# Squared deviation from the row mean: two whole-tile stores, and the sums and squares of a tile shared differently between ScalarE and VectorE

## The chip, the cores and the metric

The kernel runs on one core of a Trainium2 chip. The metric is the time of one execution in device microseconds (us), as the median of several runs; the kernel before takes 83.28 us (median of four runs, 83.21 to 83.51).

Four parts of the core matter here. VectorE (DVE) and ScalarE (ACT) compute on tiles in the on-chip memory. The queue of SyncE (SP) issues the transfers between main memory and that memory; an issue can wait for semaphores first, and what stands behind it in the queue waits with it. Sixteen DMA engines carry the transfers out. Each of them takes packets from the queue in order; here a packet is one contiguous run of one partition.

## The reference

The input `x` has 1024 rows of 4096 float32. From every element the mean of its row is subtracted, and the difference is squared. The output has the same shape and type, so 16.78 MB are read and 16.78 MB are written.

```python
def reference(x: np.ndarray, axis: int) -> np.ndarray:
    mean = np.mean(x, axis=axis, keepdims=True)
    return ((x - mean) ** 2).astype(np.float32)
```

## The kernel before

The 1024 rows are cut into two tiles of 512 rows. In a tile each of the 128 partitions holds Q = 4 consecutive rows, 16384 float32 or 64 KiB, contiguous in main memory too. Both tiles stay in the on-chip memory for the whole kernel (`io`, two buffers), so no transfer waits for a buffer.

The SP queue issues both loads at the start (L43), each of 128 runs of 64 KiB. Then a Python loop, unrolled when the program is built, goes over the two tiles and over the four rows `q` of each:

- L51, VectorE: the negated sum of the row (`neg_sum`, one value per partition).
- L54, VectorE: the sum times 1/4096 gives `neg_mean`.
- L55, ScalarE: the row is overwritten by the square of (row + `neg_mean`).
- L64, SP queue: after every second row, the store of two rows, 128 runs of 32 KiB; four stores in all, of 4 MiB each.

VectorE and ScalarE run their instructions in the order in which the program has them. A scheduler works that order out when the program is built: it puts the sum of the next row ahead of the small L54 of the row before, so that VectorE streams sums back to back and L54 never waits for the sum directly in front of it. The SP queue has the order load, load, store, store, store, store. The store of rows 0 and 1 waits for ScalarE's second square, that of rows 2 and 3 for the fourth. Both tiles are treated alike; the second one's work starts when its load has landed.

Of the kernel before, what the change touches and what calls it, by code (L numbers as in the profile page):

```python
# [2 lines left out]

os.environ.setdefault("NEURON_RT_ULTRASERVER_MODE", "4")

# [4 lines left out]

F32 = mybir.dt.float32


@with_exitstack
def kernel(
    ctx: ExitStack,
    tc: tile.TileContext,
    x: bass.AP,
    axis: bass.AP,
    out: bass.AP,  # L20
):


    nc = tc.nc

    B, D = x.shape
    P = nc.NUM_PARTITIONS
    Q = 4
    H = 2
    assert B % (P * Q) == 0  # L30
    ntiles = B // (P * Q)
    inv_d = 1.0 / float(D)

    x_t = x.rearrange("(n p q) d -> n p (q d)", p=P, q=Q)
    out_t = out.rearrange("(n p q) d -> n p (q d)", p=P, q=Q)

    io = ctx.enter_context(tc.tile_pool(name="io", bufs=ntiles))
    stats = ctx.enter_context(tc.tile_pool(name="stats", bufs=2 * ntiles * Q))

    tiles = []  # L40
    for i in range(ntiles):
        x_tile = io.tile([P, Q * D], F32)
        nc.sync.dma_start(out=x_tile, in_=x_t[i])  # L43
        tiles.append(x_tile)

    for i in range(ntiles):
        for q in range(Q):
            row = tiles[i][:, q * D:(q + 1) * D]
            neg_sum = stats.tile([P, 1], F32)
            neg_mean = stats.tile([P, 1], F32)  # L50
            nc.vector.reduce_sum(  # L51
                out=neg_sum, in_=row, axis=mybir.AxisListType.X, negate=True
            )
            nc.vector.tensor_scalar_mul(out=neg_mean, in0=neg_sum, scalar1=inv_d)  # L54
            nc.scalar.activation(  # L55
                out=row,
                in_=row,
                func=mybir.ActivationFunctionType.Square,
                bias=neg_mean,
                scale=1.0,  # L60
            )
            if q % H == H - 1:
                part = slice((q + 1 - H) * D, (q + 1) * D)
                nc.sync.dma_start(out=out_t[i][:, part], in_=tiles[i][:, part])  # L64


# [1 line left out]
_INS = ['x', 'axis']  # L68
_OUTS = [((1024, 4096), 'float32')]

_NUMBERS = {'axis': -1}


# [26 lines left out]
```

## Time and profile before

| What | us |
|---|---|
| median of four runs | 83.28 |
| the profiled execution | 83.33 |
| its span, first to last instruction | 81.5 |
| outside the span in the profiled execution | 1.8 |
| VectorE busy | 35.4 |
| ScalarE busy | 30.7 |
| one row's sum on VectorE (128x4096) | 4.411 |
| one row's square on ScalarE (128x4096) | 3.704 |
| L54 on VectorE (128x1) | 0.146 |
| issue of the two loads on the SP queue | 0.73 to 1.58 |
| first load landed (VectorE begins) | 22.71 |
| second load landed (VectorE begins again) | 42.03 |
| issue of the four stores | 39.68, 47.66, 59.00, 66.98 |

Times within the span count from its first instruction. The profile lists for each engine how long it was busy, and for the DMA queue how many packets it moved and which share of the sixteen engines' span these took. A group of instructions is given with its line, its engine, what it writes and reads, its shape, its count and its mean duration. The timeline lists the instructions in order with their starts, and in square brackets how long an engine stood idle before one of them and what ended the wait. The chain of work that ended last is followed back from the last instruction by the semaphores, as far as these show.

The trace also has a record of every single DMA packet, with its start, duration and size. These records are told here in words: the 256 packets of 64 KiB are those of the loads, the 512 of 32 KiB those of the stores, and 96 packets of 4 bytes report the end of a transfer, one for each of the six transfers on each of the sixteen engines.

### The profile page before, as it was taken

Reading aid. Unit: us, or ns where it says so; the run is one execution under the profiler, and the core shown is the slowest. Engines: PE = TensorE matmul, PEld = TensorE weight load, DVE = VectorE, ACT = ScalarE, POOL = GpSimd, SP = SyncE. Lnnn points to the kernel's source line nnn. Section 1 sums busy time; section 2 is a strip of 40 time slices with the busy share of each in tenths; the row PEclk is TensorE's granted clock in tenths of the full one; section 3 lists DMA queues with packets and bytes.
Section 4 is the critical chain, followed back from the end, with each engine's and each line's share of the span. In section 5 each row is a group of like instructions: output and inputs, shape, how many; then the busy total and the mean of one; then the engine's idle time right before and its main releaser. Section 6 shows DMA issues by size and latency. Waiting matters only on the chain.

```text
span 81.5 us, 79 instructions
## 1 busy us (share of the span) xinstructions
DVE 35.4 (43%) x16; ACT 30.7 (38%) x9; POOL 0.2 (0%) x4
## 2 busy tenths in 40 slices
DVE  0000000000089999999839999999930000000000
ACT  0000000000060005969699930978979980000000
POOL 0000000000000000000000000000000000000000
DMA  9599957999974999992997998998999899799790
GB/s 321 193 514 514 482 225 321 514 514 514 514 321 193 514 514 514 514 482 96 450 498 321 466 514 354 418 514 370 402 514 418 354 514 450 322 514 466 321 498 0
DMA packets 864, 33.55 MB, mean 411 GB/s; under 512 B 96, under 2 KB 96, under 8 KB 96
## 3 DMA queue, kind: packets, MB, share of 16 engines
q1 hardware_dynamic: 864, 33.55, 96.0%
HBM read 16.78 MB, written 16.78 MB: 411 GB/s over the span
## 4 chain that ended last, share of the span: by engine, by line
DMA 50%; DVE 22%; ACT 5%; ACTq 4%; SPq 0%; issue 0%
DMA x_tile<-in_x_dram 50%; DVE neg_sum L51 21%; ACT x_tile L55 5%; ACTq L95 4%; SPq L43 0%; DVE neg_mean L54 0%
## 5 line engine op out<-in xcount | busy, mean ns | idle before, releaser
L51 DVE TENSOR_REDUCE neg_sum<-x_tile 128x1 f32<-128x4096 f32 x8 | 35.0, 4411 | 24.3 <-DMA x_tile<-in_x_dram 24.3
L55 ACT ACTIVATE x_tile<-x_tile,neg_mean 128x4096 f32<-128x4096 f32 x8 | 29.4, 3704 | 13.5 <-DVE neg_mean L54 13.5
L55 ACT ACT_TABLE_LOAD x1 | 1.3, 1283 | 22.8 <-DMA x_tile<-in_x_dram 22.8
L54 DVE TENSOR_SCALAR neg_mean<-neg_sum 128x1 f32<-128x1 f32 x8 | 1.1, 146 | 0.0
L81 POOL MEMSET const-bfloat16-1.0<- 128x1 bf16 x1 | 0.1, 102 | 0.0
L81 POOL MEMSET const-uint8-127<- 128x1 uint8 x1 | 0.1, 102 | 0.0
L81 POOL MEMSET const-float32-0.0<- 128x1 f32 x1 | 0.1, 99 | 0.2 <-issue 0.2
L81 POOL MEMSET const-float32-1.0<- 128x1 f32 x1 | 0.1, 99 | 0.0
## 6 DMA issues: line engine op xcount, KB each, us to landing
out_dram<-x_tile SPq DMA_DIRECT2D x4, 4096.0 KB, 12.9
x_tile<-in_x_dram SPq DMA_DIRECT2D x2, 31.4
```

Source lines behind the costliest of these rows:

```text
L51: nc.vector.reduce_sum(out=neg_sum, in_=row, axis=mybir.AxisListType.X, negate=True)
L54: nc.vector.tensor_scalar_mul(out=neg_mean, in0=neg_sum, scalar1=inv_d)
L55: nc.scalar.activation(out=row, in_=row, func=mybir.ActivationFunctionType.Square, bias=neg_mean, scale=1.0,)
L81: nc = _bacc.Bacc("TRN2", target_bir_lowering=False, num_devices=1)
L95: with _tile.TileContext(nc) as tc:
```

## The change

The four stores become two. Each takes a whole tile of 8 MiB, in 128 runs of 64 KiB, and waits until all four rows of the tile are done.

The rows of a tile are shared out anew. Rows 0, 1 and 2 are summed on VectorE as before. Row 3 is summed on ScalarE: an Identity activation copies the row into a scratch buffer and adds it up (`accum_out`), and a second small activation multiplies the total by -1/4096. ScalarE then squares row 3, row 0, row 1 and the first half of row 2. VectorE squares the second half of row 2 in two passes over 2048 elements per partition: an addition of the negated mean (`tensor_scalar_add`), then a multiplication of the result with itself (`tensor_mul`).

The instructions marked `inorder` are kept in the order of the program. On VectorE each small multiplication by 1/4096 now stands directly behind the sum that it needs, and waits for it. The load of ScalarE's function table, which waited for the first tile's load in the kernel before, has no such wait after the change.

```diff
-    H = 2
+    H = D // 2
...
+    scratch = ctx.enter_context(tc.tile_pool(name="scratch", bufs=1))
...
+    inorder = tc.keep_in_program_order
+
+    def mean_on_act(row):
+        copy = scratch.tile([P, D], F32)
+        total = stats.tile([P, 1], F32)
+        neg_mean = stats.tile([P, 1], F32)
+        nc.scalar.activation(
+            out=copy, in_=row, func=ACT.Identity, scale=1.0, accum_out=total
+        )
+        nc.scalar.mul(out=neg_mean, in_=total, mul=-inv_d)
+        return neg_mean
+
+    def mean_on_dve(row):
+        neg_sum = stats.tile([P, 1], F32)
+        neg_mean = stats.tile([P, 1], F32)
+        inorder(nc.vector.reduce_sum(
+            out=neg_sum, in_=row, axis=mybir.AxisListType.X, negate=True
+        ))
+        inorder(nc.vector.tensor_scalar_mul(out=neg_mean, in0=neg_sum, scalar1=inv_d))
+        return neg_mean
+
+    def square_on_act(part, neg_mean):
+        inorder(nc.scalar.activation(
+            out=part, in_=part, func=ACT.Square, bias=neg_mean, scale=1.0
+        ))
+
     for i in range(ntiles):
-        for q in range(Q):
-            row = tiles[i][:, q * D:(q + 1) * D]
...
-            if q % H == H - 1:
-                part = slice((q + 1 - H) * D, (q + 1) * D)
-                nc.sync.dma_start(out=out_t[i][:, part], in_=tiles[i][:, part])
+        row = [tiles[i][:, q * D:(q + 1) * D] for q in range(Q)]
+        m3 = mean_on_act(row[3])
+        m0 = mean_on_dve(row[0])
+        square_on_act(row[3], m3)
+        m1 = mean_on_dve(row[1])
+        square_on_act(row[0], m0)
+        m2 = mean_on_dve(row[2])
+        square_on_act(row[1], m1)
+        square_on_act(row[2][:, :H], m2)
+        back = row[2][:, H:]
+        nc.vector.tensor_scalar_add(out=back, in0=back, scalar1=m2)
+        nc.vector.tensor_mul(out=back, in0=back, in1=back)
+        nc.sync.dma_start(out=out_t[i], in_=tiles[i])
```

More of the change, by code (lines that the diff above doesn't have):

```diff
@@ L11 @@
 F32 = mybir.dt.float32
+ACT = mybir.ActivationFunctionType
 @with_exitstack
@@ L44 @@
         tiles.append(x_tile)
-    for i in range(ntiles):
-        for q in range(Q):
-            row = tiles[i][:, q * D:(q + 1) * D]
[L49 to L61, printed above, removed]
-            if q % H == H - 1:
-                part = slice((q + 1 - H) * D, (q + 1) * D)
-                nc.sync.dma_start(out=out_t[i][:, part], in_=tiles[i][:, part])
+    inorder = tc.keep_in_program_order
[20 more added lines that the diff above has]
+        ))
+    for i in range(ntiles):
+        row = [tiles[i][:, q * D:(q + 1) * D] for q in range(Q)]
[11 more added lines that the diff above has]
+        nc.sync.dma_start(out=out_t[i], in_=tiles[i])
 _INS = ['x', 'axis']
```

## The prediction

> **What bounds the kernel now.** I read the page first: the engines' busy times beside the share of the DMA queue.
>
> ```profile
> span 81.5 us, 79 instructions
> ...
> DVE 35.4 (43%) x16; ACT 30.7 (38%) x9; POOL 0.2 (0%) x4
> ...
> DMA  9599957999974999992997998998999899799790
> ...
> DMA packets 864, 33.55 MB, mean 411 GB/s; under 512 B 96, under 2 KB 96, under 8 KB 96
> ...
> q1 hardware_dynamic: 864, 33.55, 96.0%
> ```
>
> Neither compute engine is busy for half of the span. The packets fill 96.0% of sixteen engines' time, and what is missing lies at the two ends: no packet starts before 1.7 us, and none runs after 80.4. The dips in the row of digits come from long packets being counted by their ends. The stretches with loads alone and with stores alone show that neither direction is slacker:
>
> ```profile
> 2.00:41.00 39.00, 17.71 (x8) 9.37 (x4) 0.00 (x0) 1.00 0.96 413
> 41.70:80.40 38.70, 17.71 (x8) 20.66 (x6) 0.00 (x0) 1.00 0.97 420
> ```
>
> (The columns are the stretch, its length, the busy times of VectorE, ScalarE and GpSimd, the clock, the DMA share and GB/s.) The records of single packets settle it: on each of the sixteen engines the next packet starts within some nanoseconds of the end of the one before, from the first load to the last store, also where a load passes into a store and one store into the next. So the DMA engines set the end, and computation counts only where it lets them run dry. The chain of waits on the page names DVE for 22%, because it follows semaphores and can't see that the stores stood queued.
>
> The third view is the timeline around the first store, for how nearly that happens:
>
> ```profile
> 22.71 8.74 DVE L51 TENSOR_REDUCE neg_sum<-x_tile 128x1 f32<-128x4096 f32 x2 [22.71 <-DMA x_tile<-in_x_dram]
> ...
> 35.82 4.41 DVE L51 TENSOR_REDUCE neg_sum<-x_tile 128x1 f32<-128x4096 f32 x1
> 35.94 3.71 ACT L55 ACTIVATE x_tile<-x_tile,neg_mean 128x4096 f32<-128x4096 f32 x1 [0.68 <-DVE neg_mean L54]
> 39.68 0.35 SPq L64 DMA_DIRECT2D out_dram<-x_tile  x1
> 40.15 0.27 DVE L54 TENSOR_SCALAR neg_mean<-neg_sum 128x1 f32<-128x1 f32 x2
> 40.33 3.71 ACT L55 ACTIVATE x_tile<-x_tile,neg_mean 128x4096 f32<-128x4096 f32 x1 [0.68 <-DVE neg_mean L54]
> 42.03 4.42 DVE L51 TENSOR_REDUCE neg_sum<-x_tile 128x1 f32<-128x4096 f32 x1 [1.61 <-DMA x_tile<-in_x_dram]
> ```
>
> The first store is issued at 39.68. The DMA engines finish their last load packets between 41.13 (the earliest) and 41.67 (the latest), and find store packets waiting. From the first load's issue at 0.73 to its first packet at 1.73 it took 1.00 us; for the first store it can't have been more than 41.13 - 39.68 = 1.45, as no engine stood still. I take 1.00, the only direct row, and keep 1.45 as the other end.
>
> **The stores themselves.** A load packet of 64 KiB starts 2.414 us after the one before it (median of the records), a store packet of 32 KiB 1.2095 us. Two of these make 2.419, so a 64 KiB store packet should save 0.005 if writing goes like reading. An engine carries 32 store packets now and 16 afterwards: 16 x 0.005 = 0.08. Two end reports fewer per engine, 0.006 each, bring the gain to 0.09. Two issues fewer on SP (0.34 each) gain nothing, as they lie beside running packets. As bounds: zero gain if writes have no cost per packet, and 16 x 1% of 2.414 = 0.39 lost, were long writes 1% slower than long reads; 413 against 420 GB/s in the rows above gives no hint of that.
>
> The Trainium skill speaks for far more. Its page "DMA: Bandwidth & Descriptors", section "Anatomy of one DMA — SWDGE (gpsimd) path", fits a DMA's time with a fixed 2.0 us plus its bytes, which for two stores fewer would be 4.0 us and 79.3 in all. That fit is for single transfers of another queue; here stores follow each other on an engine without a gap, so the fixed part is hidden, and I don't count it.
>
> **When the tile is released: VectorE.** It starts the first tile at 22.71. Each sum takes 4.41. The L54 behind it now waits for it: in the rows above the second one of the pair at 40.15 starts at 40.27, 0.04 after its sum's end (35.82 + 4.41 = 40.23). The next sum starts 0.06 after L54's start (31.38 to 31.44, 35.76 to 35.82). So the pitch grows to 4.41 + 0.04 + 0.06 = 4.51, where it was 4.38. The third sum ends at 22.71 + 2 x 4.51 + 4.41 = 36.14, and its mean is there 0.20 later, at 36.34 (0.04 wait, 0.15 run, 0.01 semaphore). The fourth sum, 4.4, is gone. Then come two instructions of 128x2048 that the trace doesn't have. The multiplication reads two operands and goes by the sum's row: 0.146 fixed (the 128x1 row) and 2048/4096 of the remaining 4.265, 2.28. The addition is a TENSOR_SCALAR, known only at 128x1 with 0.146; its upper end is the sum's rate again, 2.28. The two rows are equally near, one by the operation, the other by length, so I take the middle, 1.21, and keep both. Release by VectorE: 36.34 + 0.03 + 1.21 + 0.03 + 2.28 = 39.89.
>
> By the skill's page "VectorE: DVE Perf Modes", section "The perf-mode tier table (the rule you actually need)", an fp32 tensor_scalar of 2048 elements takes 1.227 us and a tensor_tensor 2.293. That would move the release by 0.03 and the total by nothing; no row here shows it.
>
> **ScalarE.** The table load (1.28) no longer waits for the first tile, and either way lies beside a sum. From 22.74: the Identity with its sum takes between 3.71 (a square) and 4.41 (VectorE's sum); I take 3.86, a square with one 128x1 instruction (0.146) on top for the total. The small multiplication lies between 0.146 (VectorE's 128x1) and 1.28 (the longest other ACT row); I take 0.20 with its wait, near the row of its shape. From 26.60 and 26.80, and with a wait of 0.03, the square of row 3 ends at 30.54. Rows 0 and 1 follow in 3.61 each (two squares take 7.31 where one takes 3.71, an overlap of 0.10), since their means are there by 27.3 and 31.8: 37.76. The half square, 0.146 + half of 3.56 = 1.93 less the overlap, ends at 39.59. The scheduler's order of the built program agrees: row 3, 0, 1, half of 2.
>
> **Sum.** The store is issued when the later engine is done, at 39.91, 0.23 after the first store of before, and its packets are ready at 40.91. The earliest DMA engine comes free at 41.13, the latest at 41.67. Nothing runs dry; the slack of the engine that ends last is 0.76. The second tile repeats it: it starts at 42.03 and takes the same 17.20, so its store is issued at 59.23, ready at 60.23; the first store's sixteen engines need 8 x 2.414 + 0.006 = 19.32 from 41.13 to 41.67, that is to 60.45 and 60.99. The slack is the same 0.76, and a delay in both tiles counts once, since a late first store moves the second one's deadline by as much. The extra waits (SP on both engines instead of one, L54 behind its sum) hold up nothing but this. So the last packet ends 0.09 before 80.40, the span, 81.54 to two places, becomes 81.45, and with the 1.79 around it the profiled execution is 83.24 instead of 83.33. That execution lay 0.05 above the median of the four runs, so for the median I predict 83.28 - 0.09 = 83.20, rounded: 0.1% less, which a measurement will hardly tell from nothing (about 0.3%, or 0.25 us, is what it tells).
>
> **Rival 1, slower: the tile is released late and the queue runs dry.** Before, half a tile was enough to start; now the longest of two chains must end. The place is the first store packet; it decides from a release after 41.67 - 1.00 = 40.67, 0.76 later than my sum, and from there each us counts in full. It exceeds 0.3% from a release after 41.01. ScalarE's upper ends (0.55 + 1.08 more) give 39.59 + 1.63 + 0.02 = 41.24, 0.57 lost, less the 0.09 gained: 83.76. The addition at its upper end gives a release at 40.98, 0.31 lost, 83.50; with an issue-to-packet time of 1.45 too, 83.95. Against it: all three values must lie near their upper ends, and an addition of up to 1.97 costs nothing.
>
> **Rival 2, faster: a store has a fixed cost that the packet records don't show.** If each dropped store gave back its issue on SP, 0.34, the time would be 82.5 with the 0.09. Against it: no gap between stores.
>
> **Rival 3, slower: long writes go worse than long reads.** At 1%: 0.39 more, 83.67. For it speaks only that no 64 KiB write is in the trace; against it, that reading 64 KiB and writing twice 32 KiB agree within 0.2%.
>
> **Rival 4: the stores don't get longer runs.** If the queue cuts a row into packets of 32 KiB, only four end reports are saved: 83.27. The loads' packets have 64 KiB, so I doubt it.
>
> **How the numbers follow.** Forecast 0.66, rival 1 0.17, rival 2 0.07, rival 3 0.04, rival 4 0.06. Faster by over 0.3%: rival 2, 0.07. Within: forecast and rival 4, 0.72. Slower: rivals 1 and 3, 0.21. The forecast's own range is 83.05 to 83.45, by the scatter of the runs (0.07 below and 0.23 above their median). To leave out no more than 2 in 10 the range goes on to the middle of rivals 1 and 3: 83.02 to 83.75.
>
> **What would show it.** After the change there should be 576 packets (256 + 256 + 64), two stores issued near 39.9 and 59.2, DVE busy 2 x (3 x 4.41 + 3 x 0.15 + 3.49) = 34.3, ACT about 35.4, and a DMA share of 96%. ScalarE and VectorE should end a tile within some 0.3 of each other. I am wrong if the first store is issued after 40.7, if a store packet of 64 KiB takes other than 2.42, or if the span moves with the queue still full.

## The result and the profile after

The changed kernel takes 83.50 us (median of 44 runs, 83.26 to 83.71); the kernel before, run beside it, 83.31 (67 runs). The ratio is 1.0022, with a 95% interval of 1.0017 to 1.0028: slower by 0.19 us, where 0.09 less was forecast. The time lies in the range given, but the sign is wrong, and many runs resolve it.

The page of the changed kernel:

```profile
span 81.7 us, 81 instructions
...
DVE 34.2 (42%) x16; ACT 34.7 (42%) x15; POOL 0.2 (0%) x4
...
DMA packets 576, 33.55 MB, mean 411 GB/s; under 512 B 64, under 2 KB 64, under 8 KB 64
...
q1 hardware_dynamic: 576, 33.55, 95.7%
...
L87 DVE TENSOR_TENSOR x_tile<-x_tile 128x2048 f32<-128x2048 f32 x2 | 4.6, 2293 | 0.1
L86 DVE TENSOR_SCALAR x_tile<-x_tile,neg_mean 128x2048 f32<-128x2048 f32 x2 | 2.6, 1286 | 0.1
```

The packets are the 576 expected, so the runs did become longer, and the engines are busy for the times that were worked out (34.3 and 35.4 expected). The DMA queue is still the bound, but its share fell from 96.0 to 95.7% while the span grew. The timeline of the first tile's end and the second tile's start:

```profile
26.56 12.80 ACT L71 ACTIVATE x_tile<-x_tile,neg_mean 128x4096 f32<-128x4096 f32 x4
...
36.06 0.15 DVE L67 TENSOR_SCALAR neg_mean<-neg_sum 128x1 f32<-128x1 f32 x1
36.25 1.29 DVE L86 TENSOR_SCALAR x_tile<-x_tile,neg_mean 128x2048 f32<-128x2048 f32 x1
37.58 2.29 DVE L87 TENSOR_TENSOR x_tile<-x_tile 128x2048 f32<-128x2048 f32 x1
39.95 0.35 SPq L88 DMA_DIRECT2D out_dram<-x_tile  x1
41.91 3.62 ACT L55 ACTIVATE copy<-x_tile 128x4096 f32<-128x4096 f32 x1 [2.56 <-DMA x_tile<-in_x_dram]
```

VectorE ends the tile at 39.87 and ScalarE at 39.36; the store is issued at 39.95 against 39.91 in the forecast. The computation did what was worked out. What differs stands in the records of the single packets around 41 us. On the sixteen engines the last load packet ends at 41.10 to 41.53, and the first store packet starts at 41.30 to 41.74. The records don't name the engine, so which start follows which end is certain only where packets stand back to back; the mean standstill does not depend on it. It is 0.21 here. Before it was 0.03: fourteen engines went on within some nanoseconds, and two stood still for about 0.2 each. From there to the last packet, end reports included, 64 KiB of store take 2.4234 on average, against 2.4223 before (pairs of 32 KiB) and 2.414 forecast. The second store shows no such gap.

So in these two executions the engines end on average at 80.24 instead of 80.11. The gap gives +0.18, the store packets 16 x 0.001 = +0.02, and a load that happened to end 0.07 earlier takes that off again. The last packet ends at 80.52 instead of 80.40, which is the 0.12 between the two profiled executions (83.45 and 83.33).

### The profile page after: what moved, and what is told of

It reads as the page before. It is cut to its first block, busy times and chain, and to the rows that moved or that the text cites. A ratio compares the mean times of both kernels' runs of the same rounds, so it can differ in the third digit from the quotient of the medians.

```text
span 81.7 us, 81 instructions
## 1 busy us (share of the span) xinstructions
DVE 34.2 (42%) x16; ACT 34.7 (42%) x15; POOL 0.2 (0%) x4
## 3 DMA queue, kind: packets, MB, share of 16 engines
q1 hardware_dynamic: 576, 33.55, 95.7%
## 4 chain that ended last, share of the span: by engine, by line
DMA 50%; DVE 21%; SPq 0%; issue 0%
DMA x_tile<-in_x_dram 50%; DVE neg_sum L64 16%; DVE x_tile L87 3%; DVE x_tile L86 2%; DVE neg_mean L67 1%; SPq L46 0%
## 5 line engine op out<-in xcount | busy, mean ns | idle before, releaser
L64 DVE TENSOR_REDUCE neg_sum<-x_tile 128x1 f32<-128x4096 f32 x6 | 26.5, 4413 | 24.6 <-DMA x_tile<-in_x_dram 24.6
L71 ACT ACTIVATE x_tile<-x_tile,neg_mean 128x4096 f32<-128x4096 f32 (+1 forms) x8 | 25.6, 3270 | 0.1
L55 ACT ACTIVATE copy<-x_tile 128x4096 f32<-128x4096 f32 x2 | 7.2, 3617 | 23.1 <-DMA x_tile<-in_x_dram 23.1
L87 DVE TENSOR_TENSOR x_tile<-x_tile 128x2048 f32<-128x2048 f32 x2 | 4.6, 2293 | 0.1
L86 DVE TENSOR_SCALAR x_tile<-x_tile,neg_mean 128x2048 f32<-128x2048 f32 x2 | 2.6, 1286 | 0.1
```

The costliest lines, as they stand in the source:

```text
L55: nc.scalar.activation(out=copy, in_=row, func=ACT.Identity, scale=1.0, accum_out=total)
L64: inorder(nc.vector.reduce_sum(out=neg_sum, in_=row, axis=mybir.AxisListType.X, negate=True))
L71: inorder(nc.scalar.activation(out=part, in_=part, func=ACT.Square, bias=neg_mean, scale=1.0))
L86: nc.vector.tensor_scalar_add(out=back, in0=back, scalar1=m2)
L87: nc.vector.tensor_mul(out=back, in0=back, in1=back)
```

## The experiments

In what follows, the gap is this mean standstill of a DMA engine between its last load packet and its first store packet. The hold is the mean time by which the load's last packet exceeds 2.418, the duration of a load packet in full flow. Both are from the packet records of one execution. Diffs are against the changed kernel unless said otherwise; unchanged lines are left out.

### Release and packet length taken apart

Four kernels. The first keeps the release of the whole tile and shortens the runs.

```diff
-        nc.sync.dma_start(out=out_t[i], in_=tiles[i])
+        for part in (slice(2 * D, 4 * D), slice(0, 2 * D)):
+            nc.sync.dma_start(out=out_t[i][:, part], in_=tiles[i][:, part])
```

> The changed kernel, but each tile is stored by two stores of 32 KiB runs, rows 2 and 3 first, both issued when all four rows are done: the release stays where it is in the changed kernel (about 39.95 us), only the packets are shorter. Theory 'late' (the queue runs dry before the first store's packets arrive): the gap of 0.05 to 0.42 us on the DMA engines ahead of the first store stays, and so does the time, 83.45 to 83.5 us (at most 0.05 less, by 16 packets of 64 KiB at 2.423 us against pairs of 32 KiB at 2.420). Theory 'long' (the longer write packets cost the time): the time falls back to that of the kernel before, 83.3 us.

Measured: 83.66 us, ratio 1.0047 (1.0034 to 1.0059).

```profile
40.01 0.82 SPq L89 DMA_DIRECT2D out_dram<-x_tile  x2
```

The gap stays, 0.20. The short packets cost 2.4335 per 64 KiB, more than the long ones. The length of the runs is thus not what made the change slower; at an equal release it saves 0.16 us, by the medians and by the packets (16 x 0.010).

The second releases rows 0 and 1 as soon as they are done:

```diff
-        nc.sync.dma_start(out=out_t[i], in_=tiles[i])
+        for part in (slice(0, 2 * D), slice(2 * D, 4 * D)):
+            nc.sync.dma_start(out=out_t[i][:, part], in_=tiles[i][:, part])
```

> The changed kernel's sharing of sums and squares, but rows 0 and 1 are stored when they are done (about 37.5 us) and rows 2 and 3 after that, in runs of 32 KiB. Theory 'late': no gap is left on any DMA engine, 83.2 to 83.3 us, not slower than the kernel before. Theory 'long': 83.3 us too. A third theory, 'contention' (ScalarE and VectorE working at once, with an addition that reads and writes on VectorE, slow the transfers): 83.5 us, since the computation is the changed kernel's.

Measured: 84.17 us, ratio 1.0110 (1.0096 to 1.0124). No theory had this. The third has long runs with an early release, by leaving row 2 unsquared:

```diff
-        square_on_act(row[2][:, :H], m2)
-        back = row[2][:, H:]
-        nc.vector.tensor_scalar_add(out=back, in0=back, scalar1=m2)
-        nc.vector.tensor_mul(out=back, in0=back, in1=back)
```

> The changed kernel without the squares of row 2 (left out on both engines, so row 2 is stored unsquared): whole-tile stores with runs of 64 KiB, released at about 37.5 us instead of 39.95. Theory 'late': the gap ahead of the first store is gone and 83.25 to 83.35 us are left, with at most 0.05 from the longer packets. Theory 'long': 83.5 us, as in the changed kernel.

Measured: 84.13 us, ratio 1.0105 (1.0087 to 1.0123). The gaps are gone in both runs (0.003 and 0.002), as 'late' expected, and yet both lose 0.9 us. The timeline shows where: the second load lands later, though nothing was done to it. For the run with short stores:

```profile
37.66 2.80 SPq L89 DMA_DIRECT2D out_dram<-x_tile  x2
42.85 3.62 ACT L55 ACTIVATE copy<-x_tile 128x4096 f32<-128x4096 f32 x1 [3.33 <-DMA x_tile<-in_x_dram]
```

and for the one with long stores:

```profile
37.65 0.35 SPq L84 DMA_DIRECT2D out_dram<-x_tile  x1
42.85 3.62 ACT L55 ACTIVATE copy<-x_tile 128x4096 f32<-128x4096 f32 x1 [5.22 <-DMA x_tile<-in_x_dram]
```

The store is issued 2.3 us earlier, and the second tile starts at 42.85 instead of 41.91. In the packet records one packet per engine is long, the load's last one: 3.29 and 3.25 on average instead of 2.42, a hold of 0.87 and 0.83. All packets before it have their normal length. The store packets after it run better than in any other kernel so far: 2.415 per 64 KiB in long runs, which is what the loads take. 'Contention' falls too, since the third kernel does less computation than the changed one and is as slow as the second.

The fourth releases later, by one more pass over the half row:

```diff
         nc.vector.tensor_mul(out=back, in0=back, in1=back)
+        nc.vector.tensor_scalar_add(out=back, in0=back, scalar1=0.0)
```

> The changed kernel with one more VectorE instruction per tile ahead of the store (adding 0.0 to the half row that it squared), 1.3 us: the release moves from 39.95 to about 41.25 us in the first tile, and as much in the second. Theory 'late': the queue is dry already, so all of it counts, once and not twice: 83.5 + 1.3 = 84.8 us, with gaps of 1.35 to 1.7 us ahead of the first store and none ahead of the second. Theory 'long': there is slack left before the release decides, so clearly less than 1.3 us is added, 83.5 to 84.3 us.

Measured: 84.04 us, ratio 1.0092 (1.0079 to 1.0105), 0.54 more than the changed kernel instead of 1.3.

```profile
41.14 0.35 SPq L89 DMA_DIRECT2D out_dram<-x_tile  x1
41.83 3.62 ACT L55 ACTIVATE copy<-x_tile 128x4096 f32<-128x4096 f32 x1 [2.54 <-DMA x_tile<-in_x_dram]
```

The store is issued when the engines are about to fall idle, and its first packets start 0.85 to 1.00 later. In the changed kernel it was issued while the engines carried the load, and its packets started 1.35 to 1.80 after the issue, although every engine was free by 1.59. So the way from issue to packet was longer where the engines were busy, and of 1.20 us of later release only 0.58 shows as a longer gap. The time lies in the range that 'long' had named, but not for its reason: no slack was left, as every engine stands still in the changed kernel already. The delay counts once, as forecast: no gap stands ahead of the second store.

### Where the best moment lies

The theories were mended to 'arrival': a store that comes early holds the load, one that comes late leaves a gap. Four more releases. The first is a complete kernel that only balances the two engines:

```diff
-    H = D // 2
+    H = 2304
```

> The changed kernel with row 2 cut at 2304 instead of 2048, so that VectorE squares 1792 elements and ScalarE 2304: both end at about 39.6 us instead of 39.36 (ScalarE) and 39.88 (VectorE), and the store is issued near 39.6, where the first store of the kernel before stood (39.68). It computes everything. Theory 'arrival': the packets of a store reach a busy DMA engine 1.35 to 1.8 us after its issue; if that lies past the load's end (41.1 to 41.5 us) the queue runs dry, if it lies well within the load's last packet that packet is held up by about 0.9 us, and the least is lost where the two meet. By it the gaps of the changed kernel go to 0 to 0.1 us and the store packets come at 2.414 to 2.420 us: 83.2 to 83.35 us. Rival 'long': 83.5 us as before this edit.

Measured: 83.22 us, ratio 0.9988 (0.9977 to 0.9999), beside 83.29 for the kernel before.

```profile
39.87 0.35 SPq L88 DMA_DIRECT2D out_dram<-x_tile  x1
42.18 3.62 ACT L55 ACTIVATE copy<-x_tile 128x4096 f32<-128x4096 f32 x1 [2.33 <-DMA x_tile<-in_x_dram]
```

The next three leave squares out to move the release:

```diff
-        square_on_act(row[1], m1)
-        square_on_act(row[2][:, :H], m2)
-        back = row[2][:, H:]
-        nc.vector.tensor_scalar_add(out=back, in0=back, scalar1=m2)
-        nc.vector.tensor_mul(out=back, in0=back, in1=back)
```

> The changed kernel without the squares of rows 1 and 2 (both stored unsquared): the store is issued at about 33.9 us in the first tile, so its packets arrive at 35.3 to 35.7, two packets ahead of the load's last one. Theory 'arrival': what is held up is the load packet in flight when the store arrives, so now it is one that starts at 33.8 to 36.9, and the loss is about 0.9 us again, 84.1 us. Rival 'order': the load's last packet is held up because a store stands behind it, whenever that came; then the packet that starts at 38.7 to 39.3 is long, the others not; the time is 84.1 us by this too, and the packet tells.

Measured: 84.48 us, ratio 1.0150 (1.0128 to 1.0172). The packets that start at 33.7 to 34.4, in flight when the store arrives, take 2.42 to 2.43. The long one is again the load's last, which starts at 38.6 to 39.3: hold 1.18. So not the packet that meets the store is held, but the last one before it, and more the longer the store has stood there: 'order' in place of 'arrival'.

```diff
-        back = row[2][:, H:]
-        nc.vector.tensor_scalar_add(out=back, in0=back, scalar1=m2)
-        nc.vector.tensor_mul(out=back, in0=back, in1=back)
```

> The changed kernel without the square of the second half of row 2 (stored unsquared): the store is issued when ScalarE is done, at about 39.4 us. Theory 'arrival': its packets come at 40.75 to 41.2 us, near the load's end: little held up, 83.2 to 83.4 us. Rival 'step' (a store that arrives anywhere in the load's last packet costs the same): 84.1 us.

Measured: 83.20 us, ratio 0.9989 (0.9978 to 0.9999). And with `row[2][:, :1024]` squared on ScalarE in place of `row[2][:, :H]`:

> As the run with the store at 39.4 us, but ScalarE squares only the first 1024 elements of row 2: the store is issued at about 38.5 us, its packets come at 39.85 to 40.3 us, in the middle of the load's last packet. Theory 'arrival' with a cost that falls towards the load's end: 83.5 to 83.9 us. Rival 'step': 84.1 us.

Measured: 83.82 us, ratio 1.0063 (1.0041 to 1.0085). The step is refuted; the hold falls towards the load's end. The rows of the timelines for 34.03, 38.59 and 39.39 (issue of the first store, and start of the second tile, in three kernels):

```profile
34.03 0.35 SPq L83 DMA_DIRECT2D out_dram<-x_tile  x1
43.07 3.62 ACT L55 ACTIVATE copy<-x_tile 128x4096 f32<-128x4096 f32 x1 [9.06 <-DMA x_tile<-in_x_dram]
```

```profile
38.59 0.35 SPq L85 DMA_DIRECT2D out_dram<-x_tile  x1
42.50 3.62 ACT L55 ACTIVATE copy<-x_tile 128x4096 f32<-128x4096 f32 x1 [3.94 <-DMA x_tile<-in_x_dram]
```

```profile
39.39 0.35 SPq L85 DMA_DIRECT2D out_dram<-x_tile  x1
42.04 3.62 ACT L55 ACTIVATE copy<-x_tile 128x4096 f32<-128x4096 f32 x1 [2.67 <-DMA x_tile<-in_x_dram]
```

The earlier the store, the later the second tile. All of it in one table, in us. The lead is from the issue of the first store to the mean end of the load, the hold taken off; the sixth column is the mean time of 64 KiB of store. All columns but the last are from one profiled execution each, the last is the median of the runs.

| Kernel | Issue | Lead | Hold | Gap | Per 64 KiB | Median |
|---|---|---|---|---|---|---|
| rows 1, 2 unsquared, long runs | 34.03 | 7.3 | 1.18 | 0.00 | 2.415 | 84.48 |
| row 2 unsquared, long runs | 37.65 | 3.7 | 0.83 | 0.00 | 2.415 | 84.13 |
| complete, short runs, early | 37.66 | 3.6 | 0.87 | 0.00 | 2.420 | 84.17 |
| quarter of row 2, long runs | 38.59 | 2.7 | 0.38 | 0.00 | 2.415 | 83.82 |
| half of row 2, long runs | 39.39 | 2.1 | 0.02 | 0.00 | 2.415 | 83.20 |
| before (short runs) | 39.68 | 1.6 | 0.01 | 0.03 | 2.422 | 83.31 |
| row 2 cut at 2304 (complete) | 39.87 | 1.4 | 0.00 | 0.15 | 2.421 | 83.22 |
| changed kernel | 39.95 | 1.3 | 0.00 | 0.21 | 2.423 | 83.50 |
| changed, short runs | 40.01 | 1.3 | 0.00 | 0.20 | 2.434 | 83.66 |
| changed, release later | 41.14 | 0.1 | 0.00 | 0.79 | 2.423 | 84.04 |

The medians follow hold plus gap, with the packets' pace as a smaller part. The loss is least at a lead of about 1.6 to 2.1, where the kernel before happened to stand; the change moved the first store 0.3 past it. The version cut at 2304 was profiled in an execution whose first load landed 0.28 later than the changed kernel's (22.84 and 22.56), so its store came 0.36 earlier as counted from there. That execution took 83.39, the longest of the twelve, so the median is better than its row shows.

The pace belongs to the gap as well, engine by engine. In the version cut at 2304, five engines have their first store packet within 3 ns of a load's end, and these ran at 2.415 or 2.416; the other eleven ran at 2.423 or 2.424. The computation beside them was the same, so it isn't the computation that slows the packets. With short runs at the changed kernel's release, one engine ran at 2.420 and fifteen at 2.432 to 2.435; there the records don't settle which of them had a gap.

### The stores alone

Against the kernel before:

```diff
-    H = 2
+    H = 4
```

> The kernel before with whole-tile stores alone (one store after the fourth row, runs of 64 KiB), the sums and squares as they were. The fourth square of the first tile ends at 47.64 us, so the store is issued there, 7.7 us after its place in the changed kernel, into an empty queue. By 'late' alone its packets start about 0.9 us later, at 48.55, and sixteen of them take 38.7: the last ends at 87.2 instead of 80.4, in all about 90.1 us; the second store (issued at 66.98, when the first one runs until 67.9) adds nothing. If the release did not matter, 83.3 us.

Measured: 90.29 us, ratio 1.0852 (1.0831 to 1.0874).

```profile
41.89 8.75 DVE L51 TENSOR_REDUCE neg_sum<-x_tile 128x1 f32<-128x4096 f32 x2 [1.60 <-DMA x_tile<-in_x_dram]
47.53 0.35 SPq L64 DMA_DIRECT2D out_dram<-x_tile  x1
```

The gap is 7.13 and counts in full. Whole-tile stores cost 7 us by themselves, through their later release, and the new sharing of sums and squares is what brings all but 0.19 of it back.

### What holds the load

Three runs asked what the hold of 0.9 belongs to. The early short stores, on ScalarE's queue (against the run with early short stores):

```diff
-            nc.sync.dma_start(out=out_t[i][:, part], in_=tiles[i][:, part])
+            nc.scalar.dma_start(out=out_t[i][:, part], in_=tiles[i][:, part])
```

> The run with the early short stores (84.17 us), but the stores are issued by ScalarE on its own queue instead of SP's, so that they don't stand behind the load in one queue. Theory 'behind' (the load's last packet is held up because a store stands directly behind it in the same queue): the hold of 0.9 us goes, the engines take store and load packets in turn, the load ends later but the total is 83.2 to 83.5 us. Rival 'turn' (the DMA engines lose the time whenever they pass from reading main memory to writing it, whatever the queue): 84.1 us or more.

Measured: 84.26 us, ratio 1.0132 (1.0115 to 1.0148), a hold of 0.84.

```profile
q1 hardware_dynamic: 288, 16.78, 48.8%
q10 hardware_dynamic: 576, 16.78, 47.2%
...
out_dram<-x_tile ACTq DMA_DIRECT2D x4, 4096.0 KB, 17.5
```

The stores have a queue of their own (q10) and still start only at 41.87 to 42.50, after the load's data. The hold is the same with a second queue, so it isn't the place in one queue. (The second tile starts at 44.06 instead of 42.85, as half of the engines report the end of the load only after their first store packet; no gap follows from it.) A small write between the two loads, against the run with early short stores:

```diff
+    warm = scratch.tile([P, 128], F32)
+    nc.gpsimd.memset(warm, 0.0)
...
+        if i == 0:
+            nc.sync.dma_start(out=out_t[1][:, 3 * D:3 * D + 128], in_=warm)
```

> The run with the early short stores (84.17 us), and a store of 64 KiB (zeros, 512 bytes in each partition, overwritten later by the right values) that stands between the two loads in the SP queue and so runs at about 21 us. Theory 'first write' (what is held up belongs to the first write of the kernel): the last packet of the first load is 0.9 us longer and that of the second is not, about 84.2 us again. Theory 'behind' (every load with a store waiting behind it loses): both last packets are held up, about 85.0 us. The 128 short packets themselves cost up to 0.2 us.

Measured: 84.63 us, ratio 1.0169 (1.0154 to 1.0184). The first load's last packet is held by 0.02, the second's by 1.13. Both theories fail: the first write as such costs nothing here, and a store waiting behind a load doesn't always hold it. 'Turn', which the run before had left standing, fails as well in its plain form: the first passage from a load to a write cost nothing. The same with a large write (`warm` of `2 * D` columns, stored to `out_t[1][:, 2 * D:4 * D]`):

> The run with a small store between the two loads, but that store now has runs of 32 KiB (4 MiB of zeros into the last two rows of the second tile, overwritten later), so it takes 8 x 1.21 = 9.7 us of every DMA engine and ends near 31.5 us. Theory 'long runs' (a load's last packet is held up whenever long store packets have stood behind it for some us): the last packet of the first load is about 1.1 us longer, and that of the second load too; 83.3 + 9.7 + 1.1 + 1.1 = 95.2 us. Rival 'end of reading' (only the very last load packet is held up, when nothing more is to be read behind it): the first load's last packet takes 2.42 us, the second's about 3.5; 94.1 us.

Measured: 94.38 us, ratio 1.1348 (1.1315 to 1.1381).

```profile
7.68 0.34 SPq L51 DMA_DIRECT2D out_dram<-warm  x1
8.07 0.43 SPq L48 DMA_DIRECT2D x_tile<-in_x_dram  x1
38.64 32.07 SPq L93 DMA_DIRECT2D out_dram<-x_tile  x4
```

The first load's last packet is held by 1.11 now, which refutes 'end of reading': another load follows. The second load's last packet, which 'long runs' expected to be held as much, is held by 0.17, though its store was issued 13.5 us ahead of the load's end. That is why the time lies nearer to the 94.1 of 'end of reading' than to the 95.2 of 'long runs'. What the hold is made of stays open. It comes where a load passes into a long store that has been waiting, on one queue or two, with runs of 32 or of 64 KiB, and in the one kernel with two such passages nearly all of it fell on the first.

## Why the prediction was wrong

**The bound** was read rightly: the DMA queue, with computation counting only at the passage from load to store.

**The release** was right to 0.04: 39.95 for 39.91 and 59.26 for 59.23; counted from the landing of the first load, which came 0.13 earlier in this execution, it was 0.17 later than worked out, so most of the agreement is luck. The two terms without a row came out at 1.29 (1.21 taken, bounds 0.15 and 2.28) and 2.29 (2.28 taken). ScalarE ended its tile at 39.36 rather than 39.59, 0.13 of it by the earlier start and the rest because the Identity with its total took 3.71 where 3.86 was taken; it had slack. The Trainium skill's figures for the two VectorE instructions ("VectorE: DVE Perf Modes", section "The perf-mode tier table (the rule you actually need)") were 1.227 and 2.293, against 1.286 and 2.293 in the profile: close for the first, exact for the second. The same addition with the constant 0.0 in place of the mean, in the kernel with the later release, took 1.227, so the 0.06 goes with the mean as an operand.

**The step that failed** is "I take 1.00, the only direct row" for the time from issue to packet, and with it "its packets are ready at 40.91 ... Nothing runs dry". With 1.35 to 1.80 in its place the packets were ready at 41.30 to 41.74, past the end of the load on every engine. The row of 1.00 was misread twice. It was the earliest of sixteen engines, while the same load's first packets started on the others up to 2.01 after the issue (1.73 to 2.74). And it came from idle engines, where the later release shows 0.85 to 1.00 again, while the store in question met busy ones. The other end, 1.45, was taken from the earliest engine too. The records of the kernel before had the right row: two engines stood still for about 0.2 each, and their first store packets came 1.69 and 1.71 after the issue. The prediction said that no engine stood still. With 1.70 its own release of 39.91 gives packets at 41.61, past all but the latest of its load ends (41.13 to 41.67).

**The second term** that failed is the gain of 0.09 from longer runs. Its rate is right, 2.415 per 64 KiB, but only where the store stands ready (four kernels of the table). Behind a gap the packets came at 2.423, so they lost 16 x 0.008 = 0.13, more than the whole gain. With the 0.18 of gap on top, the forecast of 83.20 comes to about the 83.50 measured. Against equally late short runs the longer ones did gain.

**Rival 1** named the mechanism and the place. Its deciding point, a release after 40.67, was wrong by more than 0.7 through the same 1.00, so it was given 0.17 and the forecast 0.66. Its price, every us in full, was too high: 1.20 later cost 0.58. That one of its times is the measured 83.50 is luck, as it stood for a release at 40.98.

**Rival 2**, a fixed cost per store, gets no support. Two stores and four stores released at the same moment differ by about 0.2 us, and the packet records put that into the packets' pace. The skill's fixed 2.0 us per DMA ("DMA: Bandwidth & Descriptors", section "Anatomy of one DMA — SWDGE (gpsimd) path") would have made it 4.

**Rivals 3 and 4** fall: ready store packets of 64 KiB came every 2.415, where load packets took 2.414, and there were 576 packets. (The "four end reports" of rival 4 are two per engine, as its 83.27 has it.)

**Not foreseen at all** was the other side: that an earlier release, which the forecast held to be free, costs up to 1.2 us. The slack of 0.76 was none at either side; the kernel before stood near the best moment that these runs found. What makes the early release cost so much stays open.

## What to carry to other kernels

Where transfers are the bound, read the time from an issue to its first packet on all sixteen engines and in the state that the store will meet, busy or idle; the earliest engine's value gives a slack that isn't there. Where loads passed into stores, a first store issued 2.0 us earlier than that of the kernel before cost 0.9 us, and one issued 1.5 later cost 0.7, so measure the moment by moving the release in both directions before trusting a balance. Longer runs saved 0.08 us where the store stood ready and 0.16 behind a gap, little beside what the moment of release decided. Cutting row 2 at 2304, so that both engines end together, gave a complete kernel at 0.9988 of the time before.

## What the runs showed of the hardware

- The last packet of a load was held by 0.38 to 1.18 us when the first long store had been issued 2.7 to 7.3 us ahead of the load's end, and by at most 0.02 with a lead of 2.1 or less. A second queue didn't help (0.84). A write of 512 bytes per partition held it by 0.02 only, and a second passage into long stores in one kernel by 0.17.
- A store's first packets started 0.85 to 1.00 after its issue when the engines had run idle or were about to, and 1.35 to 1.80 after it in the changed kernel, when they were carrying a load (1.18 to 1.73 with the same tile in two stores).
- Store packets of 64 KiB came every 2.415 us on an engine that had no gap ahead of the store, and every 2.423 after a gap, for the rest of the kernel. Of 32 KiB, pairs took 2.420 and 2.434. Within one execution this parted five engines from eleven.
- The addition over 2048 float32 per partition took 1.286 us on VectorE with the mean as its operand, and 1.227 with a constant.
